# Second passes with weights of 128 rows instead of 64, in a recurrence's gate products and in attention scores

## The chip, the cores and the metric

The kernel runs on one core of a Trainium2 chip. The metric is the device time of one execution in microseconds: the median of three runs of the kernel before is 1458.76 us (1458.26 to 1458.80). Where parts of an execution are spoken of, the numbers come from one execution under the hardware profiler.

## What is computed

The reference is a backbone of two layers over 512 latent tokens and 256 context tokens with 1024 features. In each layer a modulated input `u` goes through one large projection into three parallel mixers of width 512; each mixer's output is multiplied by a gate, projected to 1024 features, and summed. Two of the three mixers matter here.

Mixer B is a gated linear recurrence in both directions, after a short convolution. Its gates come from block-diagonal products: 8 blocks of 64 x 64 for each direction and gate.

```
xb = x.reshape(bsz, L, B_BLOCKS, B_BW)                      # 8 blocks of 64
r = sigmoid(einsum("blhi,hij->blhj", xb, wa) + ba)
i = sigmoid(einsum("blhi,hij->blhj", xb, wx) + bx)
a = exp(-8 * r * softplus(-lam)); h[t] = a[t] * h[t-1] + sqrt(1 - a[t]**2) * i[t] * x[t]
```

Mixer C is attention of 8 heads with 64 features each: a latent token sees a window of 8 x 16 tokens of the grid and all 256 context tokens; a context token sees the context (in the first layer only).

```
s_loc = einsum("bqhd,bsqchd->bhqsc", q_r, k_win) * scale + bias
s_ctx = einsum("bqhd,bkhd->bhqk", q_r, k_ctx) * scale
p = softmax(concatenate([s_loc, s_ctx], -1))
```

## The kernel before

All products run in float32r. Every operand x is split exactly into a high part and a low part: ACT copies the high part, DVE subtracts it from x (`split`, L297 and L298). A large product takes three passes (hi lo, lo hi, hi hi) that accumulate in PSUM (`mm3`, L346). These projections fill most of the execution. Their weights come in pieces of 512 KB over the SP queue and are split on the way (tiles `raw`, `wh`, `wl`).

Where the contraction covers 64 features only, the kernel puts the high part of an operand in one half of the 128 partitions and the low part in the other half, so that one product of 128 rows does two passes at once, and a second product does the third pass.

Branch B, `rec(t)` (t = 0 to 3, a tile of 128 features, two blocks): `X2[hh]` holds [high; low] of block hh of the convolved input, hh = 0 or 1, with the halves swapped for hh = 1. The weights `wr[0]` hold the high part of the block's matrix in both halves, `wr[1]` the low part, also in both halves, since the matrix lies twice in the input and is split as a whole. For each direction d and block hh there are two products of 128 rows, for 512 latents and for 256 context tokens (L633), and then two products of 64 rows (L635) that take the half `me` of `wr[1]` and of `X2`, where the high part of the input is. ACT reads the four halves of the result with a sigmoid (L637, L638). The latents' result stands in a PSUM bank of the tag `sc` (two buffers), the context's in one of `pv` or `tr` (one buffer each).

Branch C, `prep(t)` (t = 0 to 3, two heads): projects and rotates keys and queries, and splits them. `K2[:, hh]` holds [high; low] of the keys; `QA[hh]` holds [low; high] of the queries. `QB`, copied by ACT at L868, holds the high part of both heads, each in its own half; `QA` follows at L871 (ACT) and L872 (DVE). Then come the values' and the gate's projections. `scores(hh, j)` makes a block of scores: the queries are the weights, the keys stream. The first product has 128 rows (`QA`), the second 64 (`QB[me]` with `K2[me]`): L775 and L776 for the context's queries (j = 4, layer 0 only), L787 for blocks 0 to 2 of the latents, L789 and L790 for block 3, whose keys lie in two places. After a block of scores come a minimum (L780 or L794 and L795), an exponential with its sum (L760), the scaling by its inverse (L761, L762), the transposes (`turn`, L806), their split (L297, L298) and the products with the values (L812).

The order around these products: the steps of the attention are woven into the products of branch B's merge, one step per 3300 (layer 0) or 3000 (layer 1) streamed columns (`weave`, `tick`); what is left of a tile's steps runs after the next tile's key projection (`drain`). In branch B the order is written out in `run`: a merge step, the next tile's convolution, `rec(t)`, another merge step, the gate. Each engine works through its own queue in order.

`QB`, `QA` and `K2` lie in the scratch tile `R`; in layer 0 `QA[1]` lies in the tile `rb`, which `X2[1]` uses too.

Of the kernel before, what the change touches and what calls it, by code (L numbers as in the profile page):

```python
"""Hybrid parallel-branch backbone (gMLP / RG-LRU / neighbourhood attention), two layers, on one core.

float32 products run as three float32r passes: every operand is split exactly into a high and a low
part (x = hi + lo), and hi*lo, lo*hi and hi*hi are accumulated in float32 in PSUM.
"""
# [12 lines left out]
P = 128  # L18
# [14 lines left out]
TW = 6656  # words of the scratch area  # L33
# [7 lines left out]
def stream_order():  # L41
    """The 512 KB pieces of the weights, in the order in which the kernel uses them."""
# [30 lines left out]
# columns of the small per-partition parameters  # L73
# [10 lines left out]
def layout(inp):  # L84
    """Inputs as the kernel reads them: slices, transposes, zero padding and repeats only."""
# [4 lines left out]
    def ktiles(m):  # [K, N] -> [128, K/128, N]  # L90
        return m.reshape(m.shape[0] // P, P, m.shape[1]).transpose(1, 0, 2)
# [30 lines left out]
    # w_ada in 512 KB pieces: 256 rows of (shift, scale) of two feature tiles, or of four tiles of the gate  # L122
# [19 lines left out]
    for l in range(DEPTH):  # L142
# [9 lines left out]
        b = inp["b_ada"][l][:2048].reshape(2, 4, 2, P).transpose(3, 1, 0, 2)  # p, stage, shift/scale, tile  # L152
# [19 lines left out]
def constants():  # L172
    """Identity, rotary tables and window masks: they depend on shapes alone."""
# [13 lines left out]
    # key tiles of a query block: the columns 16j-8 .. 16j+7 and 16j+8 .. 16j+23; tile 0 of the grid holds the  # L187
    # columns 0-7 and 56-63, of which a block sees one half. The masks are the same for every row.
# [18 lines left out]
# columns of products between two steps of the attention, per layer  # L207
# [3 lines left out]
class Builder:  # L211
    def __init__(self, nc, tc, ctx, A, out):
# [32 lines left out]
        self.ssc = sb(32, "ssc")        # (stage, shift/scale, tile, stream) of the layer  # L245
        self.ua = sb(32, "ua")          # per-feature factors of the next u: scale' (tile, stream), shift'
# [10 lines left out]
    def new_v(self):  # L257
        """the area that the values take in branch C, for float32 data"""
        self.VV = self.pool.tile([P, 3584], F32, name=self.name("vv"), tag="vv", bufs=1)
        self.Vt = self.VV[:, :3072].rearrange("p (t n) -> p t n", t=6)  # L260
        self.bav, self.wst, self.kst = self.t(6 * TT, 512), self.park[:, :512], self.VV[:, 3072:]
# [8 lines left out]
    def psum(self, tag, w, bufs):  # L270
        if tag == "mmc":  # a bank of its own and one of another kind in turn
            self.half ^= 1
            if self.half:
                return self.psum(self.two, 512, 1 if self.two == "tr" else 3)[:, :256]
            return self.bank[:, :256]
# [15 lines left out]
    def order_after(self, inst, prev):  # L291
        """inst is issued behind prev (of the same engine)"""
# [14 lines left out]
    def load(self, i, dst=None):  # L307
        """fetches piece i of the stream and splits it"""
# [9 lines left out]
        if kind == "lru":  # beside the ring  # L318
# [20 lines left out]
    def mm3(self, terms, outs, first=True, last=True):  # L339
        """terms: (lhs hi, lhs lo, [(rhs hi, rhs lo) for each of outs]); first, last: or for each of outs"""  # L340
# [9 lines left out]
    def weave(self, steps, every):  # L350
        """the steps of a generator go between the products that follow, one per so many columns"""
# [15 lines left out]
    def proj(self, kind, l, t, wc, ahead=1):  # L367
        """One 128-feature tile of u @ w_in, feature-major: PSUM [128, 512] (latents), [128, 256] (context)."""
# [19 lines left out]
    def proj_tok(self, kind, l, c, toks, evac):  # L388
        """256 columns of u @ w_in for the token tiles given by toks (their slices of u)."""
# [12 lines left out]
    def start(self):  # L402
        """silu of the conditioning, the first u, and the first projections along with it"""
# [10 lines left out]
        # four projections grow with u; the context parts share banks, which start from zero  # L414
# [61 lines left out]
        with self.tc.issue_after(last.ins):  # L476
            self.constants()

    def constants(self):
        nc, V, S = self.nc, self.V, self.S  # L480
        # 4 * softplus(-lam) = 4 * (max(-lam, 0) + log1p(exp(-|lam|)))
# [21 lines left out]
    def ada_piece(self, l, i, ps, slots):  # L503
        """a quarter of the sum of 512 columns of silu(c) @ w_ada as rows (4 blocks of 128 columns, at partitions
        0, 32, 64, 96)"""
# [10 lines left out]
    def ada_cols(self, l, slots):  # L516
        """Shift and scale of the feature tiles 2s, 2s+1 for both streams, per partition, s = 0 .. 3;
        yields after every piece."""
# [52 lines left out]
    def silu(self, kind, l, t, outs, dst, tmp):  # L571
        """dst = silu(psum + b) = (x/2) (1 + tanh(x/2))"""
# [10 lines left out]
    def mixer_b(self, l, wc):  # L583
        """functions of a tile: convolution, recurrence, the tiles of y"""
# [38 lines left out]
        def rec(t):  # L623
            xc = xcs[t % 2]
            wr = [v.rearrange("p (d h n) -> p d h n", d=2, h=2) for v in self.chunk("lru", l, t)]
            for d in range(2):
                for hh in range(2):
# [6 lines left out]
                    for o, ts in outs:  # L634
                        self.T.matmul(o, wr[1][me, d, hh], X2[hh][me, ts], start=False, stop=True)  # L635
# [5 lines left out]
            # with tau = tanh(-log(a) / 2): a = 2 / (1 + tau) - 1, sqrt(1 - a^2) = 2 sqrt(tau) / (1 + tau);  # L641
            # 1 / (1 + tau) = (1 + a) / 2, from exp and a Newton step
# [9 lines left out]
            for d in range(2):  # L652
# [6 lines left out]
                V.scalar_tensor_tensor(h, w, 2.0, h, op0=ALU.subtract, op1=ALU.mult)  # -1 / (1 + tau)  # L659
# [30 lines left out]
    def mixer_c(self, l, wc):  # L690
# [11 lines left out]
        # keys in tiles of 128: grid tiles 0, 1, context, grid tiles 2, 3; for a head [kh; kl] (the second head  # L702
        # [kl; kh]) over the partitions; queries: qh of both heads, and for a head [ql; qh] (second head [qh; ql])
        K2 = self.r(0, 2 * TT).rearrange("p (h n) -> p h n", h=2)
        QB = self.r(2 * TT, n)
        if not wc:
            self.new_rb(F32)
        QA = [self.r(2 * TT + n, n), self.Rb if wc else self.r(2 * TT + 2 * n, n)]
# [17 lines left out]
        def rope(dst_views):  # L726
            """rotates z; the sum goes to permuted views"""
# [14 lines left out]
        # of a query block: where its left and right key tiles and the two of the context stand among its scores,  # L742
        # and the places of their transposed probabilities (those of two blocks for one key tile in ascending order)
        cols = [(0, 1, 2, 3), (0, 3, 1, 2), (2, 3, 0, 1), (1, 0, 2, 3)]
        slots = [(0, 1, 2, 3), (5, 4, 6, 7), (6, 1, 2, 5), (3, 4, 6, 7)]
        # after a block: (key tile, places, query blocks)
# [10 lines left out]
        def probs(ps, Pj, mn):  # L757
            """exp(-ps + mn) over its sum"""
# [5 lines left out]
        def scores(hh, j):  # L764
            """the probabilities of a block; the scores are negated"""
            me = half[hh]
            kall, kme = K2[:, hh], K2[me, hh]
# [3 lines left out]
            if j == 4:  # L771
                for i in range(2):
                    qs = slice(L + 128 * i, L + 128 * i + 128)
                    pi = ps[:, 256 * i:256 * i + 256]
                    self.T.matmul(pi, QA[hh][:, qs], kall[:, 256:512], start=True, stop=False)  # L775
                    self.T.matmul(pi, QB[me, qs], kme[:, 256:512], start=False, stop=True)  # L776
# [7 lines left out]
            for i, (q, k) in enumerate(((QA[hh][:, qs], kall), (QB[me, qs], kme))):  # L784
# [15 lines left out]
        def turn(Pj, j):  # L800
            """the transposed blocks of Pj as high and low parts"""
# [12 lines left out]
        def gather(hh, src, tmp, dst, pick):  # L814
            """both halves of the sum, times the gate"""
# [6 lines left out]
        def values(hh, j, t):  # L822
# [8 lines left out]
            if j == 1:  # L831
                pv[0] = self.psum("pv", 512, 1)
                # the second half starts from zero: its first product covers a part of it only
# [8 lines left out]
        def prep(t):  # L842
            sg = sgs[t]
            # keys
# [15 lines left out]
            # queries, negated and scaled  # L860
# [7 lines left out]
            S.copy(QB, kf[:, :n])  # L868
            for hh in range(2):
                me, it = half[hh], half[1 - hh]  # L870
                S.copy(QA[hh][it], kf[me, :n])  # L871
# [415 lines left out]
```

## Time and profile before

| | |
|---|---|
| median of three runs | 1458.76 us |
| span of the profiled execution, first to last instruction | 1456.8 us |
| PE busy | 1411.0 us, 97% |
| DVE busy | 903.8 us, 62% |
| ACT busy | 656.0 us, 45% |
| POOL busy | 253.8 us, 17% |
| branch B of layer 0, branch C of layer 0 | about 160 to 355 us, 355 to 655 us |
| branch B of layer 1, branch C of layer 1 | about 940 to 1075 us, 1105 to 1330 us |

The time of the profiled execution is known by its span only; the median of the runs is 1.96 us longer than that, and that difference is taken as what lies around the span.

How to read it: PE is the matrix engine, and PEld is the loading of its weights, which runs beside the products; DVE, ACT and POOL are the vector, scalar and general engines. A line such as L787 is one of the kernel. A product's shape is written rows*columns of its weights, then partitions x elements of what streams through. Matmuls are pipelined and their ends are modelled: the distance from one start to the next tells what a product costs, not its duration. An idle time is given with what ended it; "issue" means that no other engine did.

### The profile page before, as it was taken

How to read it: one execution, taken by the hardware profiler on the slowest of the kernel's cores; microseconds unless marked ns; L12 is line 12 of the kernel's file. 1: busy time of each engine (PE TensorE's matmuls, PEld its weight loads, DVE VectorE, ACT ScalarE, POOL GpSimd, SP SyncE). 2: the span in 40 equal slices, each digit the busy share in tenths (PEclk: the TensorE clock that was granted, in tenths of full speed). 3: DMA queues.
4: the chain of work that ended last, by engine and by line, in shares of the span. 5: the costliest groups of instructions: out<-in, count | busy, mean ns of one | idle time of the engine just before them, and what ended most of it. 6: DMA issues, size and time to landing. Idle time of an engine off the chain costs nothing.

```text
span 1456.8 us, 21334 instructions
## 1 busy us (share of the span) xinstructions
PE 1411.0 (97%) x8554; PEld 1180.4 (81%) x8554; DVE 903.8 (62%) x1526; ACT 656.0 (45%) x1032; POOL 253.8 (17%) x360
## 2 busy tenths in 40 slices
PE   6999999999999999999999989999999999999997
PEld 4898888888788888887889979877776878776797
DVE  3655476556665756562236676657887766665367
ACT  3523556763444444441132224478884454443240
POOL 0010012114112111011112162012224120202111
PEclk9999999999999999999999999999999999999999
DMA  9412121112121211127333212222222212125331
GB/s 362 140 58 66 44 68 64 65 58 74 40 63 45 64 44 57 47 93 288 120 127 124 80 44 80 88 80 80 80 69 78 69 64 78 50 72 172 118 116 59
DMA packets 38899, 130.70 MB, mean 90 GB/s; under 512 B 5136, under 2 KB 6160, under 8 KB 38800
## 3 DMA queue, kind: packets, MB, share of 16 engines
q1 hardware_dynamic: 35712, 122.36, 24.8%
q0 software_dynamic: 2800, 6.76, 1.6%
q8 instruction: 67, 1.10, 0.3%
q14 instruction: 32, 0.26, 0.1%
q10 hardware_dynamic: 288, 0.23, 0.0%
HBM read 127.22 MB, written 2.10 MB: 89 GB/s over the span
## 4 chain that ended last, share of the span: by engine, by line
PE 80%; DVE 10%; ACT 5%; issue 2%; DMA 1%; POOL 1%; SPq 0%; POOLq 0%; DVEq 0%; ACTq 0%
PE mm L346 59%; PE bank L346 7%; DVE wl L298 3%; PE sc L787 2%; PE pv L812 2%; PE tr L806 2%; ACT wh L297 2%; PE sc L346 1%; PE sc L513 1%; PE sc L635 1%; PE pv L346 1%; DMA Tar<-wa 1%; DMA raw<-ws 1%; DVE M L1138 1%; PE sc L633 1%
## 5 line engine op out<-in xcount | busy, mean ns | idle before, releaser
L346 PE MATMUL mm<-ul,wh 128*128 128x512 f32 (+1 forms) x1152 | 393.4, 377 | 5.4 <-ACT uh L446 3.1
L346 PE MATMUL mm<-uh,wl 128*128 128x512 f32 (+1 forms) x1152 | 388.9, 373 | 0.2 <-DVE wl L298 0.2
L346 PE MATMUL mm<-uh,wh 128*128 128x512 f32 (+1 forms) x1152 | 388.9, 373 | 0.0
L298 DVE TENSOR_TENSOR wl<-raw,wh 128x1024 fp32r<-128x1024 f32 (+2 forms) x151 | 206.8, 1370 | 229.1 <-ACT wh L297 227.9
L346 PEld LDWEIGHTS mm<-ul,wh 128*128 128x128 f32 x1152 | 200.2, 189 | 53.6 <-issue 8.4
L346 PEld LDWEIGHTS mm<-uh,wh 128*128 128x128 f32 x1152 | 200.3, 189 | 40.9 <-issue 3.8
L346 PEld LDWEIGHTS mm<-uh,wl 128*128 128x128 f32 x1152 | 200.2, 189 | 39.1 <-issue 2.7
L297 ACT CAST wh<-raw 128x1024 fp32r<-128x1024 f32 (+2 forms) x151 | 155.8, 1033 | 75.1 <-PE mm L346 25.3
L1030 ACT ACTIVATE Tar<-mm,hcol 128x512 f32<-128x512 f32 (+1 forms) x63 | 38.4, 635 | 141.8 <-PE mm L346 137.8
L1054 POOL TENSOR_TENSOR M<-M,Tar 128x768 f32<-128x768 f32 (+1 forms) x32 | 50.0, 1564 | 290.9 <-DVE Tar L1051 240.7
L760 ACT ACTIVATE Tar<-sc,sm 128x512 f32<-128x512 f32 (+1 forms) x80 | 51.7, 646 | 100.1 <-DVE sm L795 82.3
L346 PE MATMUL mm<-Yl,wh 128*128 128x512 f32 x228 | 81.4, 382 | 1.4 <-DVE Yl L298 1.4
L346 PE MATMUL mm<-Yh,wh 128*128 128x512 f32 x228 | 82.1, 386 | 0.0
L346 PE MATMUL mm<-Yh,wl 128*128 128x512 f32 x228 | 81.0, 380 | 0.0
L346 PE MATMUL bank<-ul,wh 128*128 128x256 f32 x248 | 70.9, 286 | 0.0
L346 PE MATMUL bank<-uh,wl 128*128 128x256 f32 x248 | 70.7, 285 | 0.0
L346 PE MATMUL bank<-uh,wh 128*128 128x256 f32 x248 | 70.5, 284 | 0.0
L297 ACT CAST vv<-tr 128x512 fp32r<-128x512 f32 (+1 forms) x88 | 48.2, 547 | 46.4 <-PE tr L806 38.4
L298 DVE TENSOR_TENSOR vv<-tr,vv 128x512 fp32r<-128x512 f32 (+1 forms) x88 | 56.0, 636 | 19.7 <-ACT vv L297 19.2
L346 PE MATMUL mm<-wl,uh 128*128 128x256 f32 x216 | 60.9, 282 | 0.0
L346 PE MATMUL mm<-wh,uh 128*128 128x256 f32 x216 | 60.4, 280 | 0.0
L346 PE MATMUL mm<-wh,ul 128*128 128x256 f32 x216 | 60.4, 280 | 0.0
(350 smaller groups left out, 2681.3 us busy)
## 6 DMA issues: line engine op xcount, KB each, us to landing
raw<-ws SPq DMA_DIRECT2D x159, 512.0 KB, 3.4
Tar<-wa SPq DMA_DIRECT2D x42, 512.0 KB, 5.0
M<-xt SPq DMA_DIRECT2D x8, 384.0 KB, 9.0
vv<-wa SPq DMA_DIRECT2D x6, 512.0 KB, 9.0
Tar<-rows POOLq DMA_DIRECT2D x6, 512.0 KB, 5.1
park<-rpb POOLq DMA_DIRECT2D x16, 188.0 KB, 3.5
vv<-xn SPq DMA_DIRECT2D x5, 512.0 KB, 4.6
raw<-lw SPq DMA_DIRECT2D x8, 256.0 KB, 2.7
```

The lines of the kernel that those rows point to most:

```text
L297: self.S.copy(h, src)
L298: self.V.tensor_tensor(l, src, h.bitcast(F32), op=ALU.subtract)
L346: self.mm = self.T.matmul(o, al if j == 1 else ah, bl if j == 0 else bh, start=(f and i == 0 and j == 0), stop=(e and i == n - 1 and j == 2))
L513: self.T.matmul(ps[32 * g:32 * g + 32, :128], sc[:, k], raw[:, kk, g], start=(k == 0), stop=(k == KT - 1))
L633: self.T.matmul(o, wr[0][:, d, hh], X2[hh][:, ts], start=True, stop=False)
L635: self.T.matmul(o, wr[1][me, d, hh], X2[hh][me, ts], start=False, stop=True)
L760: S.activation(Pj, ps, AF.Exp, bias=mn, scale=-1.0, accum_out=sm)
L787: self.T.matmul(ps, q, k[:, a:a + 512], start=i == 0, stop=i == 1)
L806: self.T.transpose(pt[:, 128 * i:128 * i + 128], Pj[:, 128 * c:128 * c + 128], ident)
L812: self.T.matmul(out, V2[:, hh, tile], v128(part)[:, a:b + 1:b - a], start=first, stop=last)
L1030: S.activation(gt[i][:, a:a + w], o, AF.Tanh, bias=self.hbcol("gm", br * 8 + d), scale=0.5)
L1054: G.tensor_tensor(m, m, gt[i][:, :n], op=ALU.add)
```

## The change

It makes every product of 64 rows in the two places one of 128 rows. In the recurrence the second pass takes the whole of `wr[1]` (low in both halves) and the whole of `X2` (high and low), so the product low times low is added. In the attention a new tile `QZ` holds, for each head, the high part of its queries in its own half and zeros in the other; the second pass takes all of `QZ[:, hh]` and all of `K2[:, hh]`, and the zeros leave the result as it was. `QZ` is a tile of its own (2 x 768 words per partition); its zeros are written once by DVE at the start, and per tile of heads ACT writes two halves where it wrote all of `QB` before. Both `QA` lie in `R` now. To make room, the scratch area of the DMAs that POOL issues is set to 4096 bytes per partition.

```diff
+        self.QZ = sb(2 * TT, "qz", F32R).rearrange("p (h n) -> p h n", h=2)
...
         with self.tc.issue_after(last.ins):
             self.constants()
+            for hh, it in ((0, slice(64, 128)), (1, slice(0, 64))):
+                V.tensor_scalar(self.QZ[it, hh], self.zero[it].bitcast(F32).to_broadcast([64, TT]), 0.0, None,
+                                op0=ALU.mult)
...
                     for o, ts in outs:
-                        self.T.matmul(o, wr[1][me, d, hh], X2[hh][me, ts], start=False, stop=True)
+                        self.T.matmul(o, wr[1][:, d, hh], X2[hh][:, ts], start=False, stop=True)
...
-        QB = self.r(2 * TT, n)
+        QZ = self.QZ
         if not wc:
             self.new_rb(F32)
-        QA = [self.r(2 * TT + n, n), self.Rb if wc else self.r(2 * TT + 2 * n, n)]
+        QA = [self.r(2 * TT + n * i, n) for i in range(2)]
...
-            me = half[hh]
-            kall, kme = K2[:, hh], K2[me, hh]
+            k = K2[:, hh]
...
-                    self.T.matmul(pi, QA[hh][:, qs], kall[:, 256:512], start=True, stop=False)
-                    self.T.matmul(pi, QB[me, qs], kme[:, 256:512], start=False, stop=True)
+                    self.T.matmul(pi, QA[hh][:, qs], k[:, 256:512], start=True, stop=False)
+                    self.T.matmul(pi, QZ[:, hh, qs], k[:, 256:512], start=False, stop=True)
...
-            for i, (q, k) in enumerate(((QA[hh][:, qs], kall), (QB[me, qs], kme))):
+            for i, q in enumerate((QA[hh][:, qs], QZ[:, hh, qs])):
...
-            S.copy(QB, kf[:, :n])
             for hh in range(2):
                 me, it = half[hh], half[1 - hh]
+                S.copy(QZ[me, hh, :n], kf[me, :n])
                 S.copy(QA[hh][it], kf[me, :n])
-                V.tensor_tensor(QA[hh][me], kf[me, :n], QB[me].bitcast(F32), op=ALU.subtract)
+                V.tensor_tensor(QA[hh][me], kf[me, :n], QZ[me, hh, :n].bitcast(F32), op=ALU.subtract)
...
-    nc = _bacc.Bacc("TRN2", target_bir_lowering=False, num_devices=1)
+    nc = _bacc.Bacc("TRN2", target_bir_lowering=False, num_devices=1, dynamic_dma_scratch_size=4096)
```

The rest of the diff takes comments out.

## Rows read from the trace of the kernel before

**Rows 1.** The page: busy time of each engine, and the chain by engine.
```profile
PE 1411.0 (97%) x8554; PEld 1180.4 (81%) x8554; DVE 903.8 (62%) x1526; ACT 656.0 (45%) x1032; POOL 253.8 (17%) x360
...
PE 80%; DVE 10%; ACT 5%; issue 2%; DMA 1%; POOL 1%; SPq 0%; POOLq 0%; DVEq 0%; ACTq 0%
```

**Rows 2.** Waits of the weight loads: total us, times, longest us.
```profile
PEld sc L787 <- issue: 14.8, 48, 0.7
```

**Rows 3.** Order of time on PE, branch B of layer 0: start us, us, instruction.
```profile
165.99 0.28 PE L346 MATMUL bank<-uh,wh 128*128 128x256 f32 x1
166.11 0.39 PE L633 MATMUL sc<-R 128*128 128x512 f32 x1
166.34 0.28 PE L633 MATMUL pv<-R 128*128 128x256 f32 x1
166.54 0.50 PE L635 MATMUL sc<-R 64*128 64x512 f32 x1
166.89 0.28 PE L635 MATMUL pv<-R 64*128 64x256 f32 x1
167.09 0.50 PE L633 MATMUL sc<-rb,R 128*128 128x512 f32 x1
167.43 0.28 PE L633 MATMUL tr<-rb,R 128*128 128x256 f32 x1
```

**Rows 4.** Order of time on PEld in the same stretch.
```profile
166.11 0.19 PEld L633 LDWEIGHTS pv<-R 128*128 128x128 f32 x1
166.54 0.18 PEld L635 LDWEIGHTS sc<-R 64*128 64x128 f32 x1 [0.24 <-issue]
```

**Rows 5.** Single lines: count, ns min/median/max, first and last start, forms.
```profile
L635 PE MATMUL sc<-R x16: 492/501/502, 166.5 to 1067.9; 64*128 64x512 f32 x16
...
L635 PE MATMUL sc<-rb,R x16: 491/494/501, 167.6 to 1069.0; 64*128 64x512 f32 x16
...
L776 PE MATMUL sc<-R x16: 379/380/382, 363.4 to 625.0; 64*128 64x256 f32 x16
...
L787 PE MATMUL sc<-R x84: 388/491/793, 365.6 to 1319.6; 64*128 64x512 f32 x48, 128*128 128x512 f32 x36
...
L789 PE MATMUL sc<-R x28: 277/379/384, 379.3 to 1323.7; 64*128 64x256 f32 x16, 128*128 128x256 f32 x12
```

**Rows 6.** Order of time on ACT and on PE, branch B of layer 0, second tile.
```profile
219.87 0.47 ACT L638 ACTIVATE vv<-tr,cols 64x256 f32<-64x256 f32 x1
...
221.51 0.28 PE L633 MATMUL tr<-rb,R 128*128 128x256 f32 x1
```

**Rows 7.** Layer 0, branch C: PE's order; a window (PE, PEld, DVE, ACT, POOL, clock).
```profile
410.63 0.39 PE L812 MATMUL pv<-vv 128*128 128x256 f32 x1 [0.46 <-DVE vv L298]
...
396.00:411.00 15.00, 14.54 (x85) 11.95 (x85) 12.39 (x25) 6.65 (x14) 4.29 (x7) 1.00 0.22 70
```

**Rows 8.** Layer 1, branch B: a window and PE's order.
```profile
955.15:991.00 35.85, 35.35 (x156) 26.78 (x155) 24.26 (x30) 34.60 (x44) 5.98 (x7) 1.00 0.24 81
...
1002.60 0.50 PE L633 MATMUL sc<-R 128*128 128x512 f32 x1 [0.52 <-ACT vv L638]
```

**Rows 9.** Layer 1, branch C: order of time on DVE and on PE.
```profile
1198.77 0.68 DVE L298 TENSOR_TENSOR vv<-tr,vv 128x512 fp32r<-128x512 f32 x1
...
1200.03 0.60 PE L806 MATMUL tr<-cst,Tar 128*128 128x128 f32 x4
...
1205.80 0.30 PE L806 MATMUL tr<-cst,Tar 128*128 128x128 f32 x1 [0.45 <-DVE Tar L762]
```

**Rows 10.** One line: the copies of 64 rows on ACT.
```profile
L871 ACT CAST R<-Tar x12: 617/620/835, 352.5 to 1287.0; 64x512 fp32r<-64x512 f32 x8, 64x768 fp32r<-64x768 f32 x4
```

**Rows 11.** DMA issues: count, KB each, median us from issue to landing.
```profile
park<-rpb POOLq DMA_DIRECT2D x16, 188.0 KB, 3.5
```

**Rows 12.** Start of branch C in layer 1: PE's order, and a window.
```profile
1109.82 1.49 PE L787 MATMUL sc<-R 128*128 128x512 f32 x2 [2.60 <-DVE R L872]
...
1109.60:1116.40 6.80, 6.58 (x13) 3.98 (x14) 5.36 (x14) 5.17 (x10) 2.56 (x6) 0.50 0.41 106
```

## The prediction

> **What bounds the kernel now.** I read the page first: PE is busy 97% of the span, DVE 62%, ACT 45%, and 80% of the chain that ended last is PE [rows 1]. That says PE sets the end, but not whether its time is well spent, because a matmul's end is modelled. So the second view is the waits of the weight loads. A line of small products stands out there: before L787, which the diff edits, the loads stood idle 14.8 us in 48 gaps, and what ended them is "issue", no other engine [rows 2]. The third view is the order of time of PE around one of them [rows 3]. A matmul there has to be read from start to start. A 512-column product of 128 rows is followed 0.23 us later (166.11 to 166.34), a 256-column one 0.12 us later (165.99 to 166.11). Around the two products of 64 rows the same steps are longer: 166.34 to 166.54 is 0.20, 166.54 to 166.89 is 0.35, 166.89 to 167.09 is 0.20, and 167.09 to 167.43, though both are of 128 rows again, is 0.34. Against 0.12, 0.23, 0.12, 0.23 the excess is 0.08 + 0.12 + 0.08 + 0.11 = 0.39 us. It falls on the two changes of the row count, into 64 and back out, half before the first product of the new kind and half behind it. The load of the first 64-row product shows why: it starts at 166.54 together with its matmul, not one product earlier as the loads of 128 rows do, and the loader was idle 0.24 us before it [rows 4]. So a run of 64-row products costs 0.39 us, however many are in it, with PE "busy" throughout.
>
> **What the edit takes from PE.** The runs are counted by line [rows 5]. L635 has 16 pairs (latents, context) on R and 16 on rb; at each of the eight steps of the recurrence two pairs of the four stand together (one run each) and two are taken apart by other products (two runs each): 16 + 32 = 48 runs. L776 has 16 products, each alone: 16. L787 has 48 of 64 rows, each alone: 48. L789 has 16, each followed by one of L790: 16. Together 128 runs, 128 x 0.39 = 50 us. By stage: branch B of layer 0 24 runs, 9.4 us; branch C of layer 0 48 runs, 18.7; branch B of layer 1 24 runs, 9.4; branch C of layer 1 32 runs (3 L787 and 1 L789 per head, 8 heads), 12.5. The products themselves keep their columns and their number, and I price a 128-row second pass like the 128-row first pass beside it, 0.23 us for 512 columns.
>
> **How much of it reaches the end.** That is the uncertain step, since a faster PE arrives earlier at work that ACT or DVE have to finish first. I take one tile of each stage and look for the product that has least room.
>
> Branch B, layer 0. The last of a step's four pairs, L633 on tr, starts at 221.51; it needs the PSUM bank that ACT L638 left at 219.87 + 0.47 = 220.34 [rows 6]. ACT works through these sigmoids without a break from the moment that the projection before them ended, so this end does not move. The room is 1.17 less some 0.05 us from a release to a start, 1.12 us; with the 0.39 of that last run, 1.5 us of a tile's 2.4 are kept. Four tiles: 6.0 of 9.4. Bounds: 0 and 9.4.
>
> Branch C, layer 0. When a tile's products run out, PE waits 0.46 us for DVE (410.63), and in the 15 us before that DVE is busy 12.39, 83% [rows 7]. I take what the last three of a tile's twelve runs give as lost there and the other nine as kept, since DVE's queue then begins earlier too: 9 x 0.39 = 3.5 per tile, 14.0 of 18.7. Bounds: half of it, 9.4, and all, 18.7.
>
> Branch B, layer 1. The tiles are shorter for PE (512 columns), while the recurrence still covers 768. ACT is busy 34.60 of 35.85 us there, and PE already waits 0.52 us for the sigmoid L638 at 1002.60 [rows 8]. There is no room, so only what ACT idled, 1.25 us in such a stretch, can come back. I take 0.5 per tile, 2.0 of 9.4. Bounds: 0 and 5 (4 x 1.25).
>
> Branch C, layer 1. PE waits 0.45 us for DVE L762 at 1205.80; at 1200.03 its transposes have 1200.03 - (1198.77 + 0.68) - 0.05 = 0.53 us of room to DVE L298 [rows 9]. Kept is at least 0.5 of a tile's 3.1; above it comes what DVE gains where it waits for PE itself. I take 1.2 per tile, 4.8 of 12.5. Bounds: 2.0 and 12.5.
>
> The sum is 6.0 + 14.0 + 2.0 + 4.8 = 26.8 us, the sums of the bounds 11.4 and 45.6. What is late next, in three of four stages, is ACT's sigmoids or DVE's splits and softmax steps.
>
> **What the edit adds.** The copy QB (L868) becomes two copies of 64 rows. Such copies took 617 ns (512 columns) to 835 ns (768 columns) at L871 [rows 10], so with the copy of 128 rows priced alike there is one more per tile, 4 x 0.83 + 4 x 0.62 = 5.8 us of ACT in all. Behind it on ACT stand the second head's QA copy and then the value bias. The first head's copy stays second in the queue, so its scores wait for nothing new; the second head's come several us later. Price 0; if that cover is gone, 5.8. The two fills of QZ with zeros go to DVE at the start, behind the table of constants; by 0.68 us for 512 columns [rows 9] some 1.0 us each, 2.0 once, in a place where PE reads PSUM filled long before. Price 0, bound 2.0. The scratch of POOL's transfers is cut to 4096 bytes. These transfers land 3.5 us after their issue [rows 11] and carry one request of 128 rows at a time. The trace of before does not show how full that area is; below 0 there is no reason, above I bound it with one landing time for each of 16 tables, 56 us on POOL, which is idle most of the span (busy 17%, [rows 1]); I take 0. QA of the second head moves from Rb into R; both were long read when it is written: 0.
>
> The profiled execution has a span of 1456.8 us; the runs' median is 1458.76, so some 2.0 us lie around it, which the change doesn't touch. 1456.8 - 26.8 = 1430.0, and 1432.0 with them.
>
> **The rivals.** (a) All is kept: the program's instructions are placed anew, and ACT's and DVE's work can move ahead with PE. For it speaks that neither is busy over 62% as a whole; against it, the waits that are there already [rows 7 to 9]. 1458.8 - 50 = 1409. (b) The cost isn't due to the row count, or widening leaves it. For it: the loads of 64 and 128 rows take the same time, 0.18 and 0.19 us [rows 4], and so do the products' columns. Then nothing is gained: 1458.8, with up to 2 us of new work. The Trainium skill (TensorE: Matmul & The Clock Gate, LDWEIGHTS) has a rule on this side, that a load's time goes by its columns, and a load of 32 rows takes as long as one of 128; by that alone the sum would be 0. The trace agrees on the loads and disagrees on the result, since the 0.39 us are gaps around the change from one kind to the other. (c) DVE and ACT hold branch C of layer 0 as they hold layer 1: kept are only 6.0 and some 4 us, 1449. (d) On the other side: new waits make PE's clock fall. It happened once around the edited lines: after a wait of 2.60 us for DVE L872 the granted clock was 0.50 (the 1.2 GHz level) from 1109.6 to 1116.4 [rows 12], at the price of half of 6.8 us, 3.4. The waits of 0.45 to 0.52 us did not do it. If the new waits grew to about 2.6 us, which is the point from which it decides, at one place in each of twelve tiles, it would be 12 x 3.4 = 41 us against 26.8: 1473. A tile's whole saving is 2.4 to 4.7 us and is spread over several waits, so I give it little.
>
> **How the numbers follow.** The forecast, 1432, has a chance of 0.74, with a range of its own from 1413 to 1447 (1458.8 less the sums of the bounds). (a) 0.12, (c) 0.08, (b) 0.03, (d) 0.03. The range reaches down to take in (a) and up to the forecast's own end: 1408 to 1447. Faster by over 0.2%, the least that a measurement of this kernel tells from no change: forecast, (a) and (c), 0.94. Same: (b), 0.03. Slower: (d), 0.03.
>
> **What would show it.** The changed profile should have no product of 64 rows at L635, L776, L787 to L790; the steps around them should be 0.23 and 0.12 us; "issue" before those loads should be gone; and waits should have grown at L633 for ACT L638, and at L806 and L812 for DVE. In layer 1's branch B the stage should be shorter by 2 us only. The forecast is wrong if the steps stay long, if those waits don't grow (then it is 1409), or if the clock row shows more stretches at 0.50.

## The result, and the profile after

The changed kernel takes 1416.03 us (median, 1414.15 to 1416.88), the kernel before, on the same chip, 1458.51: a ratio of 0.9712, with an interval of 0.9698 to 0.9726. That is 42.5 us less; the forecast was 26.8 less, 1432, with a range from 1408 to 1447. The profiled execution has a span of 1414.0 us, 42.8 less than that of before. On its page, the row that answers to the first of [rows 1] (in the changed kernel a line number is 2 to 6 higher than in the kernel before; L638 to L643 are the recurrence, L781 to L795 the scores, L299 and L300 the split):

```profile
PE 1364.6 (97%) x8554; PEld 1176.8 (83%) x8554; DVE 896.5 (63%) x1528; ACT 661.2 (47%) x1040; POOL 261.8 (19%) x360
```

PE is busy 97% as before, with 46 us less of it: what went was inside "busy". The order of time on PE at the place of [rows 3]:

```profile
164.88 0.40 PE L638 MATMUL sc<-R 128*128 128x512 f32 x1
165.11 0.28 PE L638 MATMUL pv<-R 128*128 128x256 f32 x1
165.23 0.39 PE L640 MATMUL sc<-R 128*128 128x512 f32 x1
165.46 0.27 PE L640 MATMUL pv<-R 128*128 128x256 f32 x1
165.57 0.39 PE L638 MATMUL sc<-rb,R 128*128 128x512 f32 x1
165.80 0.28 PE L638 MATMUL tr<-rb,R 128*128 128x256 f32 x1
```

From start to start it is now 0.23, 0.12, 0.23, 0.11, 0.23, where it was 0.23, 0.20, 0.35, 0.20, 0.34. So the 0.39 us per run of 64-row products are gone, and a second pass of 128 rows costs what the first does.

Where the time went is read from when the same instruction starts in both kernels. The first fence is the kernel before: the last score of layer 0 (order of time on PE), then the single lines L633 and L790 of layer 1 (count, ns min/median/max, first and last start, forms). The second is the changed kernel: first and last second passes of layer 0's scores, the first recurrence product, first score and last scores of layer 1.

```profile
644.21 0.28 PE L790 MATMUL sc<-R 64*128 64x256 f32 x1
...
L633 PE MATMUL sc<-R x8: 388/392/502, 955.0 to 1067.6; 128*128 128x512 f32 x8
...
L790 PE MATMUL sc<-R x16: 274/282/380, 1122.8 to 1323.9; 128*128 128x256 f32 x8, 64*128 64x256 f32 x8
```

```profile
L781 PE MATMUL sc<-R,qz x16: 276/279/283, 356.7 to 600.6; 128*128 128x256 f32 x16
...
618.13 0.28 PE L795 MATMUL sc<-R,qz 128*128 128x256 f32 x1
...
L638 PE MATMUL sc<-R x8: 389/447/504, 927.5 to 1038.8; 128*128 128x512 f32 x8
...
1080.90 0.76 PE L792 MATMUL sc<-R 128*128 128x512 f32 x1 [2.60 <-DVE R L877]
...
L795 PE MATMUL sc<-R,qz x8: 279/282/365, 1091.8 to 1280.5; 128*128 128x256 f32 x8
```

| from the start to | before | after | gain up to here | gain of the stage | forecast |
|---|---|---|---|---|---|
| first recurrence product, layer 0 | 166.11 [rows 3] | 164.88 | 1.2 | 1.2 | 0 |
| first second pass of scores, layer 0 | 363.4 [rows 5] | 356.7 | 6.7 | 5.5 (branch B) | 6.0 |
| last score, layer 0 | 644.21 | 618.13 | 26.1 | 19.4 (branch C) | 14.0 |
| first recurrence product, layer 1 | 955.0 | 927.5 | 27.5 | 1.4 | 0 |
| first score, layer 1 | 1109.82 [rows 12] | 1080.90 | 28.9 | 1.4 (branch B) | 2.0 |
| last score, layer 1 | 1323.9 | 1280.5 | 43.4 | 14.5 (branch C) | 4.8 |
| end of the span | 1456.8 | 1414.0 | 42.8 | -0.6 | 0 |

The first 1.2 us lie ahead of all the products edited; in the trials below that keep both second passes at 64 rows, that first recurrence product starts anywhere from 165.27 to 166.16. Both recurrences came out near the forecast. Both attentions gave more than their runs of 64 rows had cost, 18.7 us in layer 0 and 12.5 in layer 1; where the surplus comes from is said below.

### The profile page after: what moved, and what is told of

Its sections match the earlier page's. It is cut to its first block, busy times and chain, and to the rows that moved or that the text cites. A ratio compares the mean times of both kernels' runs of the same rounds, so it can differ in the third digit from the quotient of the medians.

```text
span 1414.0 us, 21346 instructions
## 1 busy us (share of the span) xinstructions
PE 1364.6 (97%) x8554; PEld 1176.8 (83%) x8554; DVE 896.5 (63%) x1528; ACT 661.2 (47%) x1040; POOL 261.8 (19%) x360
## 4 chain that ended last, share of the span: by engine, by line
PE 58%; DVE 10%; ACT 7%; issue 2%; POOL 1%; DMA 0%; POOLq 0%; DVEq 0%; ACTq 0%
PE mm L348 45%; PE bank L348 4%; PE pv L817 2%; DVE wl L300 2%; PE tr L811 2%; PE sc L792 1%; ACT wh L299 1%; ACT vv L642 1%; PE sc L518 1%; DVE Tar L768 1%; DVE vv L300 1%; DVE M L1143 1%; ACT Tar L643 0%; ACT vv L643 0%; PE sc L348 0%
## 5 line engine op out<-in xcount | busy, mean ns | idle before, releaser
L348 PE MATMUL mm<-ul,wh 128*128 128x512 f32 (+1 forms) x1152 | 389.3, 373 | 7.2 <-ACT uh L448 3.1
L300 DVE TENSOR_TENSOR wl<-raw,wh 128x1024 fp32r<-128x1024 f32 (+2 forms) x151 | 196.1, 1300 | 219.0 <-ACT wh L299 211.3
L299 ACT CAST wh<-raw 128x1024 fp32r<-128x1024 f32 (+2 forms) x151 | 155.9, 1034 | 69.4 <-PE mm L348 21.7
L1059 POOL TENSOR_TENSOR M<-M,Tar 128x768 f32<-128x768 f32 (+1 forms) x32 | 57.6, 1801 | 272.6 <-DVE Tar L1056 227.2
L300 DVE TENSOR_TENSOR vv<-tr,vv 128x512 fp32r<-128x512 f32 (+1 forms) x88 | 56.0, 637 | 15.2 <-ACT vv L299 15.0
L299 ACT CAST vv<-tr 128x512 fp32r<-128x512 f32 (+1 forms) x88 | 48.3, 549 | 34.8 <-PE tr L811 26.6
```

Source lines behind the costliest of these rows:

```text
L299: self.S.copy(h, src)
L300: self.V.tensor_tensor(l, src, h.bitcast(F32), op=ALU.subtract)
L348: self.mm = self.T.matmul(o, al if j == 1 else ah, bl if j == 0 else bh, start=(f and i == 0 and j == 0), stop=(e and i == n - 1 and j == 2))
L1059: G.tensor_tensor(m, m, gt[i][:, :n], op=ALU.add)
```

## The experiments

Times are medians; ratios are to the kernel before, run beside it on the same chip, with 95% intervals.

**One part alone: the recurrence.** Only the first edit, on the kernel before.

```diff
-  self.T.matmul(o, wr[1][me, d, hh], X2[hh][me, ts], start=False, stop=True)
+  self.T.matmul(o, wr[1][:, d, hh], X2[hh][:, ts], start=False, stop=True)
```

> The kernel before with only the recurrence's second passes made 128 rows wide (L635); scores and queries stay as they were. Engine theory of the forecast, by its terms: 6.0 us in branch B of layer 0 and 2.0 in branch B of layer 1, together 8.0 of the 18.8 us that 48 runs cost on PE, the rest turned into waits of L633 for ACT L638: 1450.5. Additions theory (the gain beyond the forecast comes from what else the change moves): the same here, 1450 to 1452. If the row count of the recurrence were free of the ACT bound: 1440.

1449.9 us, ratio 0.9949 (0.9936 to 0.9963): 7.8 us, where the forecast's terms make 8.0. This part of the sum stands, though in the profile not all of it came where it was forecast. From the first recurrence product to the first score, layer 0 is 5.8 us shorter and layer 1 only 0.6; PE's granted clock was 0.50 (the 1.2 GHz level) for 3.4 us of that stage in layer 1, up to 1038, which the kernel before doesn't have. Another 1.4 us came in layer 1's attention, which this run doesn't touch: the stretch at 0.50 of [rows 12] lasted 3.4 us there instead of 6.8.

**The other part alone: the scores.** The changed kernel with that line put back.

> The changed kernel with the recurrence's second passes back at 64 rows (L640), scores of 128 rows. Engine theory of the forecast: 14.0 + 4.8 = 18.8 us gained, 1440. Slack theory (in the attention DVE and ACT themselves wait for PE, 17.9 us in layer 0 and 13.6 in layer 1 of the trace of before, so they move ahead with PE and nothing of the 31 us is lost): all of it, about 1416 + 7.5 = 1423.5, with the waits of DVE for the scores' products cut by more than half and PE's own waits in the attention not grown.

1421.2 us, ratio 0.9759 (0.9741 to 0.9777): 36.5 us, twice the forecast's 18.8 and even more than the slack theory's 34. The two parts together make 44.3, each known to some 2 us, so they add up to the whole change. The forecast's mistake is in the attention.

**What else the change moves.** The changed kernel with both second passes at 64 rows again, reading the half of `QZ` that holds the queries.

```diff
-  for i, q in enumerate((QA[hh][:, qs], QZ[:, hh, qs])):
+  for i, (q, k) in enumerate(((QA[hh][:, qs], k), (QZ[me, hh, qs], kme))):
```

> The changed kernel with both second passes back at 64 rows, but with its new tile of queries, its zero fills, its two copies per tile, its place for the second head's queries and its smaller scratch. Forecast and slack theory: the additions are hidden, 1458.5 within 2 us. Additions theory: part of the 42 us comes from the new placement of tiles and copies and not from the row count, 1443 to 1453. If the scratch or the copies cost something, over 1461.

1457.1 us, ratio 0.9997 (0.9989 to 1.0006). The copies, the fills, the smaller scratch and the new places cost nothing and bring nothing that is clear of the noise (some 1.2 us).

**A collision of DVE and POOL.** Comparing DVE's rows showed something that the forecast had passed over: splits of weights with very different durations. Order of time on DVE and POOL in layer 0's attention, the kernel before, then the changed one:

```profile
403.48 2.82 DVE L298 TENSOR_TENSOR wl<-raw,wh 128x1024 fp32r<-128x1024 f32 x1 [0.19 <-ACT wh L297]
...
403.38 1.84 POOL L1054 TENSOR_TENSOR M<-M,Tar 128x768 f32<-128x768 f32 x1 [0.28 <-DVE Tar L1051]
```

```profile
392.64 1.23 DVE L300 TENSOR_TENSOR wl<-raw,wh 128x1024 fp32r<-128x1024 f32 x1
...
392.75 2.83 POOL L1059 TENSOR_TENSOR M<-M,Tar 128x768 f32<-128x768 f32 x1
```

Whichever starts first runs at its own pace, and the other one's time contains most of the first one's rest: POOL ends at 403.38 + 1.84 = 405.22, and DVE's 2.82 us split ends 1.08 us behind that, at 406.30, where the split alone takes 1.23. A tenth of a microsecond decides. The Trainium skill (SBUF — State Buffer, Who interferes with whom) says that a DVE operation with two inputs in SBUF contends with a POOL (GpSimd) operation that reads SBUF, that the ports they share are an exclusive lock, and that the order of issue decides who is held up; the rows agree. In the kernel before DVE loses four times in layer 0's attention (2.82 to 2.89 us) and four times in layer 1's (2.16 to 2.23); in the changed kernel never there. So the first trial was to let POOL start a little later in the kernel before:

```diff
+  if br == 1:
+      G.tensor_scalar(self.late, gt[i][:, n - 1:n], 0.5, None, op0=ALU.mult)
   G.tensor_tensor(m, m, gt[i][:, :n], op=ALU.add)
```

> The kernel before with one small operation of POOL (128x1) put ahead of each accumulation of M by POOL in the merge that runs beside the attention, so that the accumulation starts some 0.2 us later. In the trace of before four splits of weights on DVE in layer 0's attention take 2.82 to 2.89 us instead of 1.22, each having started 0.1 us behind such an accumulation, and four in layer 1's take 2.06 to 2.23; in the changed kernel DVE starts first, its splits take 1.23 us, and POOL's accumulations last longer. Collision theory: this accounts for part of the gain beyond the forecast, so that the kernel before gains 3 to 8 us by this alone, 1451 to 1455. Slack theory: DVE has room for those 1.6 us, no change, 1458.5 within 2, with the splits back at 1.2 us.

1448.8 us, ratio 0.9943 (0.9931 to 0.9956): 8.9 us, more than either theory allowed. But in the profile 3.0 of them came ahead of the first score of layer 0, where this line does nothing. There every plain pair of products (one of 512 columns, one of 256) had become faster, 347 ns instead of 353: the one word that `late` takes had moved the rings of split weights. So the run mixed two causes, and each was tried alone.

**The collision alone**, the small operation in place, so that nothing moves:

```diff
-  G.tensor_scalar(self.late, gt[i][:, n - 1:n], 0.5, None, op0=ALU.mult)
+  G.tensor_scalar(gt[i][:, n - 1:n], gt[i][:, n - 1:n], 1.0, None, op0=ALU.mult)
```

> The run before this kind took one word of memory more for its small POOL operation, which moves the rings of split weights by one word, and its plain 512-column products in layer 0 stand 228.5 ns apart instead of 233 (in layer 1 233.5 instead of 229). Here the small operation works in place on one column of the merge's result (times 1.0), so nothing moves. Collision theory: the four collisions per layer are gone, worth steps of 0.7 us each in layer 0 and up to 0.5 in layer 1, 3 to 5 us in all: 1453 to 1455. Placement theory: all of the 8.9 us was the moved word, 1457.7 within 2. If both 512-column steps and collisions change again, 1449.

1453.98 us, ratio 0.9979 (0.9969 to 0.9988): 3.9 us. The same place in this kernel's order of time:

```profile
403.40 1.23 DVE L298 TENSOR_TENSOR wl<-raw,wh 128x1024 fp32r<-128x1024 f32 x1 [0.18 <-ACT wh L297]
...
403.60 2.72 POOL L1056 TENSOR_TENSOR M<-M,Tar 128x768 f32<-128x768 f32 x1
```

All eight splits are short again. The collision theory holds, and the collisions are worth 4 us of the kernel before.

**The collision put back into the changed kernel**, by giving POOL its accumulation in two parts, the first one earlier.

> The changed kernel with POOL's accumulation of M beside the attention cut in two in layer 0, the first part issued 0.4 us earlier, as soon as the first 512 columns are there, so that it is under way when DVE comes to its split of weights, as it was in the kernel before. Nothing moves in memory. Collision theory: the four long splits of layer 0 are back and cost 2 to 4 us of the gain, 1418 to 1420. Slack theory: the changed kernel has room for them, 1416 within 2.

1414.2 us, ratio 0.9699 (0.9686 to 0.9713), no slower than the changed kernel. The trial missed its aim: DVE still started first in all places but one (a split of 2.21 us at 615.7), and POOL's parts waited instead. It says nothing on what a collision would cost there.

**The moved word alone**, on the changed kernel:

```diff
+  self.pad = sb(1, "pad")
   self.QZ = sb(2 * TT, "qz", F32R).rearrange("p (h n) -> p h n", h=2)
```

> The changed kernel with one unused word ahead of the new tile, so that this tile and the rings of split weights move by one word. Placement theory: the 512-column steps in layer 0 fall from 233 to about 228.5 ns and those in layer 1 rise from 229 to 233; from the curve of the run with the moved word some 3 us in branch B and 2 to 3 us in branch C of layer 0 and 1 between the layers, less 1 to 2 in layer 1: 1409 to 1413. If that step came with the small POOL operation and not with the word: 1416 within 2.

1411.9 us, ratio 0.9688 (0.9675 to 0.9701). The order of time on PE, first and last product of one undisturbed stretch of layer 0 (209 products, 512 and 256 columns in turn) and of one of layer 1 (68 products of 512), the changed kernel, then the one with the word:

```profile
174.32 0.28 PE L348 MATMUL mm<-ul,wh 128*128 128x256 f32 x1
...
211.05 0.28 PE L348 MATMUL bank<-uh,wh 128*128 128x256 f32 x1
...
1341.41 0.39 PE L348 MATMUL mm<-ul,wh 128*128 128x512 f32 x1
...
1356.75 0.40 PE L348 MATMUL mm<-Yh,wh 128*128 128x512 f32 x1
```

```profile
173.80 0.28 PE L349 MATMUL mm<-ul,wh 128*128 128x256 f32 x1
...
209.86 0.28 PE L349 MATMUL bank<-uh,wh 128*128 128x256 f32 x1
...
1336.86 0.39 PE L349 MATMUL mm<-ul,wh 128*128 128x512 f32 x1
...
1352.49 0.39 PE L349 MATMUL mm<-Yh,wh 128*128 128x512 f32 x1
```

In layer 0 a pair takes 36.73 / 104 = 353 ns, with the word 36.06 / 104 = 347. In layer 1 a product takes 15.34 / 67 = 229 ns, with the word 15.63 / 67 = 233. The placement theory holds in both directions. That stretch of layer 0 varies by itself: in runs without the word a pair there takes 349 to 353 ns. The next two of that layer, from the last product of a tile's recurrence to the first of the next, vary less: 39.08 and 30.60 us in the changed kernel, 38.37 and 30.05 with the word. The placement is no part of the gain: there the additions alone have 39.40 and 30.91 us, as the kernel before.

**Had DVE room in the attention?** The forecast had given up a quarter of layer 0's attention and more of layer 1's because PE waited for DVE at the end of a tile. Against that stands a view that it hadn't used, what DVE itself waits for. Waits of DVE in branch C of layer 0 and then layer 1 (total us, times, longest), before and after:

```profile
DVE sm L794 <- PE sc L787: 11.6, 15, 1.7
DVE sm L794 <- PE sc L790: 3.3, 4, 1.2
DVE sm L780 <- PE sc L776: 3.0, 3, 1.0
...
DVE sm L794 <- PE sc L787: 11.5, 11, 3.3
```

```profile
DVE sm L799 <- PE sc L792: 3.7, 6, 1.5
DVE sm L799 <- PE sc L795: 2.3, 4, 0.8
DVE sm L785 <- PE sc L781: 1.1, 3, 0.4
...
DVE sm L799 <- PE sc L792: 4.3, 11, 0.7
```

DVE stood 11.6 + 3.3 + 3.0 = 17.9 us in layer 0 waiting for scores, and 7.1 in the changed kernel. To see whether this was room, work was added to DVE, one operation of 256 columns in each of the 80 blocks:

```diff
   V.reciprocal(sm, sm)
+  V.tensor_scalar(self.late, self.cos[:, :256], 0.5, None, op0=ALU.mult)
```

> The kernel before with one more operation of DVE, 256 columns, some 0.3 us, in each of the 80 blocks of the attention ahead of the scaling (24 us of DVE in all, 14 in layer 0); its tile takes 256 words, for which the scratch is cut as in the changed kernel. Slack theory: in the trace of before DVE waits 17.9 us (layer 0) and 13.6 us (layer 1) for the scores' products, so most of this is taken up, 0 to 6 us slower: 1458 to 1464. Engine theory of the forecast (DVE at its limit in the attention already, room of some 0.5 us per tile): about 20 us slower, 1478.

> The same 80 operations of DVE in the changed kernel, where DVE's waits for the scores' products are down to 7.1 and 4.7 us. Slack theory: some 24 - 12 = 12 us slower, 1424 to 1432, with PE's waits for DVE in the attention grown by about that. Engine theory: again about 20 us or more, 1436 or more. If DVE still had as much room as before: 1416 to 1419.

1457.1 us (ratio 1.0003, 0.9991 to 1.0014) and 1416.7 us (0.9724, 0.9704 to 0.9743). Both numbers mean nothing for the question: the operations depended on nothing in their block, and in both kernels they ran from 55 to 108 us. But the first shows that the new tile and the smaller scratch, which the last run has too, change nothing by themselves. The last run ties each to its block.

```diff
   V.reciprocal(sm, sm)
+  V.tensor_scalar(self.late[:, :w], Pj[:, :w], sm, None, op0=ALU.mult)
```

> The run before of this kind put its 80 operations of DVE where they could run ahead of time: they ran from 56 to 108 us, long before the attention, and tell nothing about it. Here each reads the block's own exponentials and their sum, so it can only run within its block, ahead of the scaling. 0.29 us each, 23 us in all, 14 in layer 0 and 9 in layer 1. Kernel before. Slack theory (DVE waits 17.9 and 13.6 us for the scores' products there): 0 to 6 us slower, 1457 to 1463. Engine theory of the forecast (DVE holds the tile's end, room of some 0.5 us per tile): some 20 us slower, 1477.

1457.9 us, ratio 1.0002 (0.9993 to 1.0011). The added line, and the stage windows of branch C of layers 0 and 1 (us; busy of PE, PEld, DVE, ACT, POOL; clock, DMA share, GB/s):

```profile
L764 DVE TENSOR_SCALAR late<-Tar,sm x80: 334/353/1504, 367.2 to 1328.7; 128x256 f32<-128x256 f32 x80
...
355.00:655.00 300.00, 295.19 (x1687) 246.09 (x1687) 203.12 (x446) 131.34 (x262) 35.62 (x61) 1.00 0.17 56
1105.00:1330.00 225.00, 221.49 (x1106) 174.53 (x1105) 168.44 (x351) 107.89 (x200) 40.06 (x70) 0.98 0.22 70
```

The operations take 353 ns at the median, and DVE is busy 203.12 + 168.44 = 371.6 us in the two stages, 350.1 in the same windows of the kernel before: 21 us of new work within the attention (each overlaps its neighbours a little), at no cost that the runs show. In the profile layer 0's attention is 1.5 us longer from the first score to the last, and layer 1's 0.6 shorter; the eight long splits are still there. The sum of DVE's work did not hold the attention of the kernel before; the engine theory falls, the slack theory stands. That doesn't mean that DVE has room at every place: the collisions, 1.6 or 1.0 us at one place in each of eight tiles, cost 3.9 us.

**Is it ACT's load that holds the recurrence in layer 1?** The high copies of the weights fetched in that stage were taken from ACT and given to POOL, and in a second kernel to DVE.

```diff
-  self.split(h, lo, r)
+  (self.G.tensor_copy if self.offact else self.S.copy)(h, r)
+  self.V.tensor_tensor(lo, r, h.bitcast(F32), op=ALU.subtract)
```

> The changed kernel with the high copies of the weights that are fetched in branch B of layer 1 made by POOL and not by ACT (six or seven copies of some 1.03 us per tile), results the same. ACT theory: in that stage PE waits 10.9 us, 7.1 of it at L638 for the sigmoids of ACT, so with some 6 us less per tile on ACT PE gets 6 to 9 us back: 1407 to 1410. Rival: POOL's copies hold up DVE's splits as its accumulations do beside the attention, or come later than ACT's, and PE waits for the weights instead: 1416 or slower.

> The same copies on DVE, which was busy 73% of that stage and waited 10.6 us for ACT's copies in it. ACT theory: 6 to 9 us back as with POOL, 1407 to 1410, if a copy takes DVE no more than the 1.0 us it takes ACT. Rival: DVE, with some 27 us more, becomes what PE waits for in that stage: 1416 or slower.

On POOL 1420.5 us (ratio 0.9748, 0.9726 to 0.9770), on DVE 1415.65 (0.9719, 0.9699 to 0.9739): slower by some 4 to 5 us, and the same. The stage window of the changed kernel and of the one with the copies on DVE (columns as above), and then that one's waits of the weight loads in the same stage (its lines are 2 higher):

```profile
912.60:1050.00 137.40, 130.54 (x606) 104.56 (x605) 97.92 (x119) 113.83 (x151) 27.89 (x27) 1.00 0.23 79
```

```profile
911.90:1049.50 137.60, 130.54 (x598) 104.32 (x597) 111.28 (x139) 99.36 (x135) 31.84 (x28) 0.99 0.24 79
...
PEld sc L640 <- ACT vv L645: 7.4, 8, 2.9
PEld pv L640 <- ACT vv L645: 3.2, 4, 1.8
```

ACT has 14.5 us less to do, and the loads still wait for its sigmoids as long as in the changed kernel (below). So less work on ACT alone doesn't free this stage. The run is no clean test, though: DVE has 13.4 us more to do, and ACT's waits for DVE grew from 6.1 to 11.7 us, so a wait that DVE hands on isn't ruled out. The copies on POOL lost time in another way: there ACT waited 17.8 us for DVE's product of the gate and the scans' sum (L684 in the changed kernel, where it waited 3.2), and PE's granted clock was 0.96 over the stage, with three stretches near 0.50 that the changed kernel doesn't have.

## Why the prediction was right, and where it was not

The time lies in the stated range, near its lower end: the two attentions, forecast at 18.8 us together, gave 33.9. Of the forecast's signs, the steps of 0.23 and 0.12 us came, and so did the longer waits at L633; those at L806 and L812 did not grow, taken together, which it had named as a sign that it was wrong.

**The price of a run of 64 rows: right.** 0.39 us, half before and half behind, gone with the row count (start to start above). The rival that the row count is not the cost falls, with the additions alone at 0.9997. Its rule, that a load's time goes by columns (the Trainium skill, TensorE: Matmul & The Clock Gate, LDWEIGHTS), agrees with the loads of 0.18 and 0.19 us in [rows 4] and still says nothing on the gaps around them. The Trainium skill has a sentence that fits these: changing the tiling mode drains TensorE (TensorEngine Tiling (Array Packing), Key Properties). It gives no price, and no run here shows that a drain is what happens in the gaps.

**Branch B of layer 0: right to the step.** The forecast said that the fourth pair's L633 could move ahead by 1.12 us and would then stand at the end of ACT's sigmoid. ACT's and PE's order of time at the place of [rows 6], after:

```profile
217.41 0.47 ACT L643 ACTIVATE vv<-tr,cols 64x256 f32<-64x256 f32 x1
...
217.94 0.39 PE L638 MATMUL tr<-rb,R 128*128 128x256 f32 x1
```

The sigmoid ends at 217.88 and the product starts 0.06 later. From the tile's first product, 213.63 before and 211.17 after (2.46 earlier), to this one the gain rose from 2.46 to 221.51 - 217.94 = 3.57, by 1.11 us.

**Branch B of layer 1: the size near, the reason half right at most.** Waits of the weight loads in that stage, before and after:

```profile
PEld sc L633 <- ACT vv L638: 2.3, 3, 1.1
...
PEld tr L633 <- ACT vv L638: 1.0, 1, 1.0
```

```profile
PEld sc L638 <- ACT vv L643: 6.0, 8, 2.2
PEld tr L638 <- ACT vv L643: 3.0, 4, 1.8
...
PEld pv L638 <- ACT vv L643: 1.9, 3, 0.9
```

3.3 us became 10.9, which takes back 7.6 of the 9.4 that the switches gave. But "ACT is busy 34.60 of 35.85 us, so there is no room" was not the whole reason: with 14.5 us less on ACT, and 13.4 more on DVE, the waits stayed (7.4 + 3.2 there, and 1.5 on `tr`). What is most likely is the order of steps within a tile, product, sigmoids one after the other, then the next product in the same bank, with too few other products between them. That is argued from the rows; a kernel with more products between the pairs was not tried.

**The attention: this step failed.** "I take what the last three of a tile's twelve runs give as lost" (14.0 of 18.7) and "kept is at least 0.5 of a tile's 3.1 ... I take 1.2" (4.8 of 12.5) came out at 19.4 and 14.5. Waits of PE in branch C of layer 0: before, after, and in the kernel before with the collision alone taken out:

```profile
PE tr L806 <- DVE Tar L762: 1.7, 2, 0.8
PE pv L812 <- DVE vv L298: 1.4, 3, 0.5
```

```profile
PE pv L817 <- DVE vv L300: 1.3, 3, 0.4
PE tr L811 <- DVE Tar L768: 0.9, 1, 0.9
```

```profile
PE tr L806 <- DVE Tar L762: 1.2, 1, 1.2
```

The waits that [rows 7, 9] showed were there, and they did not grow (in layer 1 they were 1.6 us before, and 0.7 after). The forecast read them as an engine at its limit. In the kernel before they were largely the collision's work: with it alone taken out, the three waits at L812 are gone, that of 0.46 us at 410.63 among them, and so are the four at L806 in layer 1 (1.6 us together), that at 1205.80 among them. And the rest of DVE's work stands in a chain that begins with a product, so the chain moved ahead with PE; DVE's own waits for scores, 17.9 us, were the room, and 21 us more work on DVE cost nothing. The busiest stretch that I took as the measure, 83% from 396 to 411, contained the collision at 403.48 too: 1.6 of its 12.39 busy us were beyond what the split takes alone. Rival (a), everything is kept, was right for the attention and wrong for the recurrence.

**The surplus.** Layer 0's attention had 18.7 us of switches and gave 19.4; layer 1's had 12.5 and gave 14.5. What is above comes from two things that are luck of timing and no merit of the edit. The first are the eight collisions, which the kernel before pays 3.9 us for and the changed kernel doesn't, since DVE is 0.1 us ahead of POOL there instead of behind it. With them alone taken out, the kernel before has its first and last score at 362.73 and 642.01 in layer 0 and at 1105.08 and 1318.07 in layer 1; against 363.19 to 644.21 and 1109.82 to 1323.91 that is 1.7 and 1.1 us shorter. The second is the clock. After the 2.60 us wait for L877, which is there as in [rows 12], the stretch at 0.50 was 3.4 us and not 6.8, which is worth up to half of the difference, 1.7 us. It isn't the row count that does it: the additions alone, with 64 rows, have that stretch at 3.4 us too, and their stage is 1.3 us shorter. Less these, the row count gave 19.4 - 1.7 = 17.7 of 18.7 us and 14.5 - 1.1 - 1.7 = 11.7 of 12.5: nearly all, and not more. That is an estimate from single profiles; the trial to put the collision back missed. Between the layers too the stretch is 3.4 us where it was 6.8 (850.18 to 857.01), behind a wait of 3.65 us (3.66 before). Stage windows at 0.50 (columns as above; clock third from the end), after:

```profile
824.37:827.78 3.41, 3.18 (x15) 3.18 (x16) 3.31 (x5) 0.00 (x0) 3.35 (x2) 0.50 0.02 5
1080.37:1083.78 3.41, 2.88 (x7) 2.33 (x8) 2.04 (x3) 3.34 (x6) 1.44 (x3) 0.50 0.17 44
1295.41:1298.82 3.41, 3.41 (x21) 2.14 (x22) 0.69 (x1) 0.00 (x0) 0.54 (x1) 0.50 0.74 265
```

The third is new, behind the last score, and takes some of that back (the -0.6 of the table). It follows a wait of 2.21 us for DVE's split `Yl` that was 1.35 us in the kernel before, where the clock stayed. That is what rival (d) described, at one place; the additions alone have that wait too (2.22 us) and a stretch at 0.50 behind it, so it isn't the wider products that make it. There are three stretches for two ahead of the kernel's last work, which the forecast had named as a sign too, but they last 10.2 us together and not 13.6. Elsewhere no new wait of that length came around the edited lines.

**The additions: right**, 0.9997, the scratch among them.

## What to carry to other kernels

A change of the number of rows cost PE 0.39 us a run here, and its busy share hid it; read matmuls from start to start, and pad a short second pass with zeros or with a harmless extra product where the memory is there. Before you write off a gain because PE waits for an engine, look at what that engine itself waits for: an engine that waits for PE in the same stage has room in sum, if not at every place, and its work at the end of a chain moves along. Try it with added work that is tied to the place, and look at where the added work ran before the time is read. An engine's busy time may be another engine's: durations of the same operation that differ twofold are worth a look before any share is worked out from them.

## What was new about the hardware

One word of placement changed the pace of plain products: 353 to 347 ns for a pair in layer 0, 229 to 233 ns for a product in layer 1, worth 4 us between the medians of 1416.0 and 1411.9. The kernel with the word is the fastest one measured; its interval just touches that of the changed kernel. What moved were the tile of queries, the rings of split weights and what lies behind them. The kernel before has no such tile of queries, and the word of `late` took a pair there from 353 to 347 ns too, so it isn't that tile; which of the others matters, and why layer 1 goes the other way, stays open. And a DVE subtraction and a POOL addition that overlap by their starts within 0.1 us cost the later one 1.6 us on DVE or 1.0 on POOL (2.82 against 1.23, 2.83 against 1.84).
